# Two score products one place later, every sparse-attention softmax urgent, and wider value products in a hybrid decoder layer

## The chip, the cores and the metric

The kernel runs on one core of one Trainium2 chip. The metric is the device time of one execution in microseconds (us). The kernel before takes 330.74 us, the median of three runs (330.63 to 331.23). A lower time is better.

## The reference, cut to what matters

One decoder layer over 256 tokens of width 1024, in float32. Two causal attention mixers work side by side on the same normed input, and their outputs are concatenated into one output projection. Behind them stand a SwiGLU block, a gated per-layer embedding and a last norm, which the change does not touch.

```python
a = rmsnorm(h, g_attn[i])
proj = a @ w_in[i]
qa, ka, va, qi, ki, wi, qb, kb, vb = jnp.split(proj, offs, axis=-1)
...
y_a = dsa_attention(qa, ka, va, qi, ki, wi).reshape(B, L, W_DSA)
y_b = moba_attention(qb, kb, vb).reshape(B, L, W_MOBA)
h = h + jnp.concatenate([y_a, y_b], axis=-1) @ w_out[i]
f = rmsnorm(h, g_ffn[i])
h = h + (jax.nn.silu(f @ w_gate[i]) * (f @ w_up[i])) @ w_down[i]
```

Mixer A (called DSA) first scores every past key with a small indexer, keeps the 64 best keys of each query, and lets 8 query heads of 64 numbers attend to them. All 8 heads share one key head and one value head:

```python
rel = jax.nn.relu(jnp.einsum('bthd,bsd->bths', qib, k_idx).astype(jnp.float32))
score = jnp.einsum('bth,bths->bts', wb, rel)
score = jnp.where(causal[None], score, -jnp.inf)
_, idx = lax.top_k(score, top)
...
logits = jnp.where(valid[:, :, None, :], logits, -jnp.inf)
prob = jax.nn.softmax(logits, axis=-1).astype(v.dtype)
return jnp.einsum('bthk,btkd->bthd', prob, vs)
```

Mixer B (MoBA) is, at this length, plain causal attention of 8 heads, each with keys and values of its own.

## The kernel before, in words

TensorE (PE) runs in the order in which the program is written. The other engines run in an order that a planner settles when the kernel is built: by priority, which follows the order of the program text, and work written under `urgent()` comes 100 places earlier. On the chip each engine then takes its instructions in that settled order, one after the other.

A weight matrix comes in chunks of 1 MB. ScalarE (ACT) casts a chunk to `hi` (line 131), VectorE (DVE) subtracts to get the rest `lo` (line 159), and every product with weights is three matmuls, hi by hi, hi by lo and lo by hi (`mm3`, lines 176 to 178, or line 313 for the input projection).

The attention is cut into units. A unit is a kind (a for DSA, b for MoBA), a query tile of 128 tokens (t = 0 or 1) and the heads it takes: `A[0]` is tile 0 with all 8 heads and 128 keys, `A[1]` and `A[2]` are tile 1 with 4 heads each and 256 keys. A unit has three steps:

- `qk`: the score products (line 453) into two banks, one for even heads (e = 0) and one for odd heads (e = 1), and right behind them the softmax: DVE adds the mask and takes the minimum (line 471), ACT takes the exponential and its sum (line 477), DVE the reciprocal (481). Tile 0 is then scaled on DVE (484), tile 1 on ACT (488).
- `tp`: PE transposes the probabilities of one e (495), ACT copies them to `pT` (497).
- `pv`: products of the values with `pT` (509), even heads into partitions 0 to 63 of the bank and odd heads into 64 to 127. ACT and DVE take the result out as `yH` and `yL` (516, 517), which the output projection reads.

The mask of a DSA unit comes from `topk(t)` on DVE: eight rounds of the maximum of 8 (429) and its removal (430), and then lines 431 and 432 write `dmask`. `A[1]` and `A[2]` need the mask of tile 1.

These steps are put between the matmuls of the output projection by a plan: `at_tick(key, ...)` hangs functions on a place, and `tick(key)` runs them there. Place ("wb", n) lies behind the n-th group of six output products with MoBA's part of the weights (n = 0 to 3 for tile 0, 4 to 7 for tile 1), place ("wa", n) behind the n-th group of six with DSA's part for tile 0. Before, the softmaxes of `B[0]`, `A[1]` and `A[2]` are urgent (`first`, line 524), that of `A[0]` is not.

```python
        first = (B[0], A[1], A[2])
...
        at_tick(("wb", 0), A[0].qk, lambda: tp_rope(4, 1, qaT))
        at_tick(("wb", 2), B[2].pv, A[1].qk)
        at_tick(("wb", 5), tp(A[0], 0), tp(A[0], 1))
        at_tick(("wb", 6), A[0].pv, A[2].qk)
        at_tick(("wa", 0), tp(A[1], 0), tp(A[1], 1))
        at_tick(("wa", 1), A[1].pv)
```

`tp_rope(4, t, qaT)` transposes the rotated DSA queries of a tile on PE, and ACT copies them to `qaT` (381, 383). The score products of that tile read this copy.

Of the kernel before, what the change touches and what calls it, by code (L numbers as in the profile page):

```python
# [16 lines left out]
P = 128  # L17
# [45 lines left out]
def layer_kernel(  # L63
# [26 lines left out]
    def aux(name):  # L90
        return ps_aux.tile([P, NQ], F32, tag="aux", name=name)

    chunks, off = [], 0
    for kind, k0, nk, width, _, _ in CHUNKS:
        n = P * nk * width
# [84 lines left out]
    def urgent():  # L180
        return tc.high_priority(offset=URG)

    def tsl(t):
        return slice(t * P, (t + 1) * P)
# [87 lines left out]
    with actx:  # L272
# [105 lines left out]
        def transpose4(src, dstT, t, name):  # L378
            pt = aux(name)
            for b in range(4):  # L380
                nc.tensor.transpose(pt[:, b * P : (b + 1) * P], src[:, b * P : (b + 1) * P], ident)
            with urgent():
                nc.scalar.copy(dstT[:, :, tsl(t)], pt.rearrange("p (b n) -> p b n", b=4))
# [12 lines left out]
        def tp_rope(g, t, dstT):  # L396
            transpose4(ropes[(g, t)].rearrange("p h d -> p (h d)"), dstT, t, f"tr{g}{t}")
# [36 lines left out]
        class Unit:  # L434
# [57 lines left out]
            def tp(self, e):  # L492
                pt = aux(f"pt_{self.name}{e}")
                for b in range(4):
                    nc.tensor.transpose(pt[:, b * P : (b + 1) * P], self.pr[e][:, b * P : (b + 1) * P], ident)
                with urgent():
                    nc.scalar.copy(self.pT[:, e, :], pt)

            def pv(self):
                t, nb = self.t, self.nb  # L500
                ns = t + 1
                pv = aux(f"pv_{self.name}")
                for i in range(nb):
                    for s in range(ns):
                        for e in range(2):
                            hd = self.h0 + 2 * i + e
                            v = va[:, s, :] if self.kind == "a" else vb[:, s, hd * 64 : (hd + 1) * 64]
                            b = i * ns + s
                            nc.tensor.matmul(
                                pv[64 * e : 64 * e + 64, i * P : (i + 1) * P],  # L510
                                v, self.pT[:, e, b * P : (b + 1) * P], start=s == 0, stop=s == ns - 1,
                            )
                k0 = (0 if self.kind == "a" else 4) + self.h0 // 2
                src = pv[:, : nb * P].rearrange("p (k n) -> p k n", k=nb)
                with urgent():
                    nc.scalar.copy(yH[:, k0 : k0 + nb, tsl(t)], src)
                    nc.vector.tensor_tensor(
                        yL[:, k0 : k0 + nb, tsl(t)], src, yH[:, k0 : k0 + nb, tsl(t)].bitcast(F32), op=ALU.subtract
                    )

        B = [Unit("b", t, h0) for t, h0 in ((0, 0), (1, 0), (1, 4))]
        A = [Unit("a", t, h0) for t, h0 in ((0, 0), (1, 0), (1, 4))]

        first = (B[0], A[1], A[2])

        def at_tick(key, *fs):
            plan.setdefault(key, []).extend(fs)
# [13 lines left out]
        at_tick(("pp", 0), lambda: topk(1))  # L541
        at_tick(("pp", 1), tp(B[1], 0), tp(B[1], 1))
        at_tick(("pp", 3), B[1].pv, tp(B[2], 0), tp(B[2], 1), lambda: tp_rope(4, 0, qaT))
        at_tick(("wb", 0), A[0].qk, lambda: tp_rope(4, 1, qaT))
        at_tick(("wb", 2), B[2].pv, A[1].qk)
        at_tick(("wb", 5), tp(A[0], 0), tp(A[0], 1))
        at_tick(("wb", 6), A[0].pv, A[2].qk)
        at_tick(("wa", 0), tp(A[1], 0), tp(A[1], 1))
# [31 lines left out]
        qaT = at.tile([P, 4, 256], F32, tag="qaT", name="qaT")  # L580
# [36 lines left out]
        i = 0  # L617
# [28 lines left out]
    def trn(t, c, XHn, XLn, name):  # L646
        hg = hgs[(t, c)]
        pt = aux(f"ht_{name}{t}{c}")
        for b in range(4):
            nc.tensor.transpose(pt[:, b * P : (b + 1) * P], hg[:, b * P : (b + 1) * P], ident)  # L650
        pv = pt.rearrange("p (b n) -> p b n", b=4)
        kk = slice(4 * c, 4 * c + 4)
        with urgent():
            nc.scalar.copy(XHn[:, kk, tsl(t)], pv)
            nc.vector.tensor_tensor(XLn[:, kk, tsl(t)], pv, XHn[:, kk, tsl(t)].bitcast(F32), op=ALU.subtract)
# [48 lines left out]
    def hid_split(b, t, w, ht, H, L):  # L704
        nb = w // P
        pv = ht[:, :w].rearrange("p (s b i) -> p b s i", s=4, b=nb)
        kk = slice(4 * b, 4 * b + nb)
        hH = H[:, kk, tsl(t)].rearrange("p b (s i) -> p b s i", s=4)
        nc.scalar.copy(hH, pv)
        nc.vector.tensor_tensor(  # L710
            L[:, kk, tsl(t)].rearrange("p b (s i) -> p b s i", s=4), pv, hH.bitcast(F32), op=ALU.subtract
        )
# [232 lines left out]
```

## Time and profile before

| | |
|---|---|
| time, median of 3 runs | 330.74 us |
| the profiled execution | 330.68 us |
| its span, first to last instruction | 328.9 us |
| PE busy | 318.7 us, 97% of the span |
| DVE busy | 230.5 us, 70% |
| ACT busy | 181.5 us, 55% |
| granted TensorE clock, mean | 0.994 of full speed |

PE is at work nearly everywhere, so a wait of PE is time lost, and work of ACT or DVE costs only where PE waits for it. In rows of a timeline the first number is the start in us, the second the duration; the time in brackets is how long the engine had been idle, and what ended that. Matmuls and other instructions overlap their neighbours a little, so what one costs in a row of like ones is the step from its start to the next start, which is smaller than its duration.

### The profile page before, as it was taken

To read this page: it belongs to the slowest core of one execution; us is meant where nothing else is said; L and a number is where in the kernel's file an instruction comes from. 1 tells how busy PE (TensorE), PEld (TensorE's weight loads), DVE (VectorE), ACT (ScalarE), POOL (GpSimd) and SP (SyncE) were. 2 spreads that over 40 slices of the span, in tenths; PEclk is the share of its full clock that TensorE was granted. 3 is DMA by queue.
4 is the path that set the end of the run, shared out by engine and by line. 5 is a ranking of instruction groups with operands and counts; after the bars stand their busy time and mean duration, and the time that the engine had idled before them with its cause. 6 is when DMAs were issued, how large, how long until landed. Compare 5 with 4: busy or idle time off the path is not lost.

```text
span 328.9 us, 4397 instructions
## 1 busy us (share of the span) xinstructions
PE 318.7 (97%) x1589; PEld 260.0 (79%) x1589; DVE 230.5 (70%) x459; ACT 181.5 (55%) x294; POOL 6.1 (2%) x16
## 2 busy tenths in 40 slices
PE   8999999998989999999999999999999999999991
PEld 7888887776767788888888888888878888888891
DVE  4969999999966697547745756467573525279894
ACT  5966356898678495334543455335544333338533
POOL 2001000000000000000000000000000000000030
PEclk9999999999999999999999999999999999999997
DMA  7995948231503346677568476776858564551011
GB/s 257 417 392 221 369 157 299 87 129 40 217 5 125 129 148 251 241 271 259 170 253 295 149 286 236 262 248 212 250 169 313 210 209 175 190 192 66 0 64 65
DMA packets 19749, 66.00 MB, mean 201 GB/s; under 512 B 3344, under 2 KB 9488, under 8 KB 13456
## 3 DMA queue, kind: packets, MB, share of 16 engines
q1 hardware_dynamic: 19584, 65.53, 55.7%
q8 instruction: 12, 0.20, 0.3%
q10 hardware_dynamic: 144, 0.20, 0.2%
q14 instruction: 9, 0.07, 0.1%
HBM read 61.53 MB, written 4.19 MB: 200 GB/s over the span
## 4 chain that ended last, share of the span: by engine, by line
PE 83%; DVE 9%; ACT 6%; issue 0%
PE g L313 14%; PE ff L178 12%; PE ff L176 12%; PE ff L177 12%; PE wd L177 6%; PE wd L176 6%; PE wd L178 6%; PE pg L178 2%; PE pg L177 2%; PE pg L176 2%; DVE lo L159 2%; ACT pr_b L477 2%; DVE score L430 2%; ACT pr_a L477 2%; DVE m L429 1%; ACT hi L131 1%
## 5 line engine op out<-in xcount | busy, mean ns | idle before, releaser
L159 DVE TENSOR_TENSOR lo<-raw,hi 128x1024 fp32r<-128x1024 f32 (+1 forms) x99 | 116.8, 1207 | 62.8 <-ACT hi L131 62.8
L131 ACT CAST hi<-raw 128x1024 fp32r<-128x1024 f32 (+1 forms) x99 | 98.6, 1042 | 79.6 <-PE wd L178 31.9
L176 PE MATMUL ff<-hi,FH 128*128 128x512 f32 x176 | 68.7, 390 | 0.0
L178 PE MATMUL ff<-hi,FL 128*128 128x512 f32 x176 | 68.5, 389 | 0.0
L177 PE MATMUL ff<-lo,FH 128*128 128x512 f32 x176 | 68.5, 389 | 0.0
L178 PEld LDWEIGHTS ff<-hi,FL 128*128 128x128 f32 x176 | 33.0, 188 | 7.0
L177 PEld LDWEIGHTS ff<-lo,FH 128*128 128x128 f32 x176 | 33.0, 188 | 6.9
L176 PEld LDWEIGHTS ff<-hi,FH 128*128 128x128 f32 x176 | 33.0, 188 | 6.7
L177 PE MATMUL wd<-lo,hidH 128*128 128x512 f32 x88 | 35.1, 399 | 0.0
L176 PE MATMUL wd<-hi,hidH 128*128 128x512 f32 x88 | 34.9, 397 | 0.0
L178 PE MATMUL wd<-hi,hidL 128*128 128x512 f32 x88 | 34.5, 392 | 0.0
L313 PE MATMUL g<-hi,XH 128*128 128x512 f32 x64 | 25.5, 403 | 0.0
L313 PE MATMUL g<-hi,XL 128*128 128x512 f32 x64 | 24.8, 393 | 0.0
L313 PE MATMUL g<-lo,XH 128*128 128x512 f32 x56 | 21.7, 393 | 0.0
L176 PEld LDWEIGHTS wd<-hi,hidH 128*128 128x128 f32 x88 | 16.5, 188 | 4.4 <-DVE hid L749 0.3
L178 PEld LDWEIGHTS wd<-hi,hidL 128*128 128x128 f32 x88 | 16.5, 188 | 4.0
L177 PEld LDWEIGHTS wd<-lo,hidH 128*128 128x128 f32 x88 | 16.5, 188 | 3.7
L744 ACT ACTIVATE sg<-ff,f_y 128x512 f32<-128x512 f32 (+1 forms) x12 | 7.8, 647 | 15.0 <-PE ff L178 15.0
L749 DVE SCALAR_TENSOR_TENSOR hid<-ff,f_y,sg 128x512 f32<-128x512 f32 (+1 forms) x12 | 8.4, 703 | 10.5 <-PE ff L178 9.4
L313 PEld LDWEIGHTS g<-hi,XH 128*128 128x128 f32 x64 | 12.0, 188 | 3.1 <-issue 0.7
L313 PEld LDWEIGHTS g<-hi,XL 128*128 128x128 f32 x64 | 12.0, 188 | 2.6
L176 PE MATMUL pg<-hi,UH 128*128 128x512 f32 (+1 forms) x40 | 14.0, 349 | 0.0
(200 smaller groups left out, 441.7 us busy)
## 6 DMA issues: line engine op xcount, KB each, us to landing
raw<-in_w_dram SPq DMA_DIRECT2D x48, 1024.0 KB, 5.2
a<-in_xa_dram SPq DMA_DIRECT2D x8, 354.5 KB, 6.0
hidd<-hidb SPq DMA_DIRECT2D x11, 256.0 KB, 2.7
hidt<-hidd SPq DMA_DIRECT2D x44, 64.0 KB, 3.1
raw_g<-in_w_dram SPq DMA_DIRECT2D x2, 512.0 KB, 7.7
h<-in_x_dram SPq DMA_DIRECT2D x1, 1024.0 KB, 11.2
raw<-in_w_dram SPq DMA_DIRECT2D x2, 256.0 KB, 4.3
raw<-in_w_dram SPq DMA_DIRECT2D x1, 512.0 KB, 8.3
```

Of the source, the lines that this page charges most:

```text
L131: nc.scalar.copy(hi[:, o : o + step], raw[:, o : o + step])
L159: nc.vector.tensor_tensor(lo[:, o:e], raw[:, o:e], hi[:, o:e].bitcast(F32), op=ALU.subtract)
L176: nc.tensor.matmul(ps, aH, wH, start=start, stop=False)
L177: nc.tensor.matmul(ps, aH, wL, start=False, stop=False)
L178: nc.tensor.matmul(ps, aL, wH, start=False, stop=stop)
L313: nc.tensor.matmul(pss[t][:, :width], aT[:, k, tsl(t)], wT, start=k == 0 and n == 0, stop=k == KD - 1 and n == 2,)
L429: nc.vector.max(m8, s[:, :n])
L430: nc.vector.match_replace(s[:, :n], m8, s[:, :n], SENT)
L477: nc.scalar.activation(pr[:, sl], lg[:, sl], AF.Exp, bias=mn[:, j : j + 1], scale=-1.0, accum_out=su[:, j : j + 1])
L744: nc.scalar.activation(sg[:, :w], ps[:, :w], AF.Silu, scale=rf[t])
L749: nc.vector.scalar_tensor_tensor(hid[:, :w], up, rf[t], pgu[("s", t)][:, :w], op0=ALU.mult, op1=ALU.mult)
```

## The change

Three edits. The score products of `A[0]`, with the transposes of the second half of the DSA queries behind them, move from place ("wb", 0) to ("wb", 1), and those of `A[1]` from ("wb", 2) to ("wb", 3). The softmax of `A[0]` becomes urgent too. And `pv` of a DSA unit multiplies the values of a key tile with all its query blocks of one e in one matmul: `A[0]` has 2 matmuls of 512 columns where it had 8 of 128, `A[1]` and `A[2]` have 4 of 256 columns each where they had 8 of 128.

```diff
@@ -500,15 +500,17 @@
                 pv = aux(f"pv_{self.name}")
-                for i in range(nb):
+
+                wide = nb if self.kind == "a" else 1
+                for i in range(0, nb, wide):
                     for s in range(ns):
                         for e in range(2):
                             hd = self.h0 + 2 * i + e
                             v = va[:, s, :] if self.kind == "a" else vb[:, s, hd * 64 : (hd + 1) * 64]
-                            b = i * ns + s
+                            pT = self.pT[:, e, :].rearrange("p (i s n) -> p s i n", i=nb, s=ns)[:, s, i : i + wide, :]
                             nc.tensor.matmul(
-                                pv[64 * e : 64 * e + 64, i * P : (i + 1) * P],
-                                v, self.pT[:, e, b * P : (b + 1) * P], start=s == 0, stop=s == ns - 1,
+                                pv[64 * e : 64 * e + 64, i * P : (i + wide) * P],
+                                v, pT, start=s == 0, stop=s == ns - 1,
                             )
@@ -521,7 +523,7 @@
-        first = (B[0], A[1], A[2])
+        first = (B[0], *A)
@@ -541,8 +543,9 @@
-        at_tick(("wb", 0), A[0].qk, lambda: tp_rope(4, 1, qaT))
-        at_tick(("wb", 2), B[2].pv, A[1].qk)
+        at_tick(("wb", 1), A[0].qk, lambda: tp_rope(4, 1, qaT))
+        at_tick(("wb", 2), B[2].pv)
+        at_tick(("wb", 3), A[1].qk)
```

On DVE the edits change what stands between the softmax of `A[0]` and the end of the search for tile 1. Before, the last rows of the two run mixed; `m_1` and `score` with number 630 belong to the search of tile 1, `lg_a_1000` is a masked score of `A[0]`, odd heads, and `pr_a_989` its probabilities of even heads:

```order
L471 ISA lg_a_1000,mn_a_985<-qk_a_976,dmask 128x128
L471 ISA mn_a_985 128x1
L429 MAX m_1_876<-score_630 128x8
L481 RECIPROCAL rc_a_987<-su_a_986 128x4
L471 ISA lg_a_1000,mn_a_985<-qk_a_976,dmask 128x128
L471 ISA mn_a_985 128x1
L430 MATCH_REPLACE score_630<-m_1_876,score_630 128x256
L484 TENSOR_TENSOR pr_a_989<-pr_a_989,rc_a_987 128x512
L431 TENSOR_SCALAR dmask<-score_630 128x256
L517 TENSOR_TENSOR yL<-pv_b_1039,yH 128x2x128
L432 TENSOR_TENSOR dmask<-dmask,cadd 128x256
L471 ISA lg_a_1000,mn_a_985<-qk_a_976,dmask 128x128
```

Now all eight line-471 pairs of `A[0]` stand ahead of this piece, and from there DVE goes on as follows; `pr_a_995` and `pr_a_1007` are the probabilities of `A[0]`, even and odd heads, and `lg_a_1065` is the first masked score of `A[1]`:

```order
L429 MAX m_1_876<-score_630 128x8
L481 RECIPROCAL rc_a_993<-su_a_992 128x4
L430 MATCH_REPLACE score_630<-m_1_876,score_630 128x256
L484 TENSOR_TENSOR pr_a_995<-pr_a_995,rc_a_993 128x512
L429 MAX m_1_876<-score_630 128x8
L430 MATCH_REPLACE score_630<-m_1_876,score_630 128x256
L481 RECIPROCAL rc_a_993<-su_a_992 128x4
L519 TENSOR_TENSOR yL<-pv_b_1039,yH 128x2x128
L484 TENSOR_TENSOR pr_a_1007<-pr_a_1007,rc_a_993 128x512
L431 TENSOR_SCALAR dmask<-score_630 128x256
L432 TENSOR_TENSOR dmask<-dmask,cadd 128x256
L471 ISA lg_a_1065,mn_a_1062<-qk_a_1056,dmask 128x256
```

Two rounds of the search, both reciprocals of `A[0]` and both of its scalings (line 484) now stand between its scores and the mask of tile 1.

On ACT the order changes at the softmax of `A[2]`, between the value products of `A[0]` and those of `A[1]`. Before, with `pr_a_1135` and `pr_a_1144` the probabilities of `A[2]` and `pT_a_1077` the copy of the transposed probabilities of `A[1]`:

```order
L516 CAST yH<-pv_a_1114 128x4x128
L477 ACTIVATE pr_a_1135,su_a_1132<-lg_a_1134,mn_a_1131 128x256 x2
L477 ACTIVATE pr_a_1144,su_a_1132<-lg_a_1143,mn_a_1131 128x256
L488 ACTIVATE pr_a_1135<-pr_a_1135,rc_a_1133 128x256 x2
L477 ACTIVATE pr_a_1144,su_a_1132<-lg_a_1143,mn_a_1131 128x256
L497 COPY pT_a_1077<-pt_a_1173 128x512
L488 ACTIVATE pr_a_1144<-pr_a_1144,rc_a_1133 128x256 x2
L497 COPY pT_a_1077<-pt_a_1179 128x512
L131 CAST hi_1027<-raw_1025 128x1024 x2
```

Now, with `pr_a_1129` and `pr_a_1138` the probabilities of `A[2]` and `pT_a_1083` the copy of `A[1]`:

```order
L518 CAST yH<-pv_a_1114 128x4x128
L131 CAST hi_966<-raw_964 128x1024
L477 ACTIVATE pr_a_1129,su_a_1126<-lg_a_1128,mn_a_1125 128x256 x2
L477 ACTIVATE pr_a_1138,su_a_1126<-lg_a_1137,mn_a_1125 128x256 x2
L131 CAST hi_1027<-raw_1025 128x1024
L488 ACTIVATE pr_a_1129<-pr_a_1129,rc_a_1127 128x256 x2
L488 ACTIVATE pr_a_1138<-pr_a_1138,rc_a_1127 128x256 x2
L497 COPY pT_a_1083<-pt_a_1167 128x512
L497 COPY pT_a_1083<-pt_a_1173 128x512
```

A weight cast now stands on either side of `A[2]`'s exponentials, and both copies for `A[1]` stand behind all four scalings of `A[2]`.

## Rows read from the trace of the kernel before

**Rows 1.** Two lines of the page: busy time, share of the span and instructions of each engine, and the shares of the chain that ended last.

```profile
PE 318.7 (97%) x1589; PEld 260.0 (79%) x1589; DVE 230.5 (70%) x459; ACT 181.5 (55%) x294; POOL 6.1 (2%) x16
...
PE 83%; DVE 9%; ACT 6%; issue 0%
```

**Rows 2.** Waits of PE between 74 and 113 us, and, the last line, the only wait of its weight loads (PEld) from 115 us to the end. Columns: who waited, the releaser, us in total, times, longest us.

```profile
PE qk_a L453 <- ACT qaT L383: 1.0, 1, 1.0
PE pv_a L509 <- ACT pT_a L497: 0.9, 1, 0.9
...
PEld wd L176 <- DVE hid L749: 0.3, 1, 0.3
```

**Rows 3.** Timeline of PE at the scores of `A[0]` (16 records, 8 matmuls of 128 columns) and of `A[1]` (8 records, 4 matmuls of 256 columns).

```profile
79.44 0.39 PE L178 MATMUL wo<-hi,yL 128*128 128x512 f32 x1
80.84 1.16 PE L453 MATMUL qk_a<-idxT,qaT 64*128 64x128 f32 x16 [1.01 <-ACT qaT L383]
81.93 0.66 PE L381 MATMUL tr<-ident,qa 128*128 128x128 f32 x4
82.34 0.48 PE L176 MATMUL wo<-hi,yH 128*128 128x512 f32 x1
...
86.29 1.14 PE L453 MATMUL qk_a<-idxT,qaT 64*128 64x256 f32 x8
87.35 0.50 PE L176 MATMUL wo<-hi,yH 128*128 128x512 f32 x1
```

**Rows 4.** Timeline of PE at the value products of `A[0]` (94.95), `A[1]` (102.72) and `A[2]` (108.11).

```profile
93.69 0.39 PE L178 MATMUL wo<-hi,yL 128*128 128x512 f32 x1
94.95 1.57 PE L509 MATMUL pv_a<-pT_a,va 128*64 128x128 f32 x16 [0.87 <-ACT pT_a L497]
96.46 1.13 PE L453 MATMUL qk_a<-idxT,qaT 64*128 64x256 f32 x8
...
102.72 1.61 PE L509 MATMUL pv_a<-pT_a,va 128*64 128x128 f32 x16
104.26 0.50 PE L176 MATMUL wo<-hi,yH 128*128 128x512 f32 x1
...
108.11 1.09 PE L509 MATMUL pv_a<-pT_a,va 128*64 128x128 f32 x16
109.13 0.50 PE L176 MATMUL wo<-hi,yH 128*128 128x512 f32 x1
```

**Rows 5.** Timeline of DVE, from the last weight subtraction ahead of the softmax of `A[0]` to the first masked scores of `A[1]`.

```profile
81.89 1.21 DVE L159 TENSOR_TENSOR lo<-raw,hi 128x1024 fp32r<-128x1024 f32 x1
...
83.08 0.41 DVE L430 MATCH_REPLACE8 score<-m,score 128x256 f32<-128x256 f32 x1
83.41 0.28 DVE L471 CUSTOM_DVE_ANT_0 lg_a<-qk_a,dmask 128x128 f32<-128x128 f32 x1
...
83.61 0.42 DVE L429 MAX8 m<-score 128x8 f32<-128x256 f32 x1
...
86.24 0.16 DVE L481 RECIPROCAL rc_a<-su_a 128x4 f32<-128x4 f32 x1
...
86.90 0.68 DVE L484 TENSOR_TENSOR pr_a<-pr_a,rc_a 128x512 f32<-128x512 f32 x1
...
88.04 0.41 DVE L432 TENSOR_TENSOR dmask<-dmask,cadd 128x256 f32<-128x256 f32 x1
...
88.59 0.42 DVE L471 CUSTOM_DVE_ANT_0 lg_a<-qk_a,dmask 128x256 f32<-128x256 f32 x1
...
88.94 0.42 DVE L471 CUSTOM_DVE_ANT_0 lg_a<-qk_a,dmask 128x256 f32<-128x256 f32 x1
```

**Rows 6.** Timeline of ACT from the first query copy to the second copy of `A[1]`.

```profile
80.16 0.63 ACT L383 COPY qaT<-tr 128x512 f32<-128x512 f32 x1
...
83.73 0.40 ACT L477 ACTIVATE pr_a<-lg_a,mn_a 128x128 f32<-128x128 f32 x1 [0.52 <-DVE mn_a L471]
...
89.59 0.50 ACT L477 ACTIVATE pr_a<-lg_a,mn_a 128x256 f32<-128x256 f32 x1
...
90.08 0.39 ACT L477 ACTIVATE pr_a<-lg_a,mn_a 128x128 f32<-128x128 f32 x1
...
90.47 0.89 ACT L488 ACTIVATE pr_a<-pr_a,rc_a 128x256 f32<-128x256 f32 x2
...
93.39 1.03 ACT L131 CAST hi<-raw 128x1024 fp32r<-128x1024 f32 x1
94.33 1.06 ACT L497 COPY pT_a<-pt_a 128x512 f32<-128x512 f32 x2
95.28 1.05 ACT L131 CAST hi<-raw 128x1024 fp32r<-128x1024 f32 x1
...
101.35 0.56 ACT L497 COPY pT_a<-pt_a 128x512 f32<-128x512 f32 x1
...
102.62 0.57 ACT L497 COPY pT_a<-pt_a 128x512 f32<-128x512 f32 x1
```

**Rows 7.** Busy time of each engine in three stretches; the columns are named in the view as: us, PE busy (instructions), PEld, DVE, ACT, POOL, granted clock of PE, DMA share, GB/s.

```profile
74.00:84.00 10.00, 8.99 (x70) 7.25 (x69) 10.00 (x32) 8.12 (x16) 0.00 (x0) 1.00 0.31 102
...
320.00:325.00 5.00, 1.71 (x15) 1.50 (x13) 4.40 (x13) 2.67 (x4) 0.00 (x0) 1.00 0.13 48
325.00:329.00 4.00, 0.00 (x0) 0.00 (x0) 0.00 (x0) 0.00 (x0) 0.00 (x0) 0.51 0.36 133
```

## The prediction

> **What bounds the kernel now.** I read the page first: PE is busy for 318.7 of 328.9 us, and the chain that ended last is PE's for 83% [rows 1]. So the time is PE's work plus PE's waits. Next the waits of PE: in the attention part two are left, 1.0 us of the scores of `A[0]` for `qaT` and 0.9 us of the value products of `A[0]` for `pT`; from 115 us to the end there is one wait of 0.3 us [rows 2]. Two things follow. The change can win little more than these 1.9 us, and what it loses before 115 us arrives at the end in full, as no later wait is there to swallow it. Then the timelines of PE, DVE and ACT around the two places. One wait is not in the list of waits: the value products of `A[1]` take 1.54 us to the next start (102.72 to 104.26), those of `A[2]`, with both copies there, 1.02 us (108.11 to 109.13) [rows 4]. The missing 0.5 us are the second copy of `A[1]`, which starts at 102.62 [rows 6] while PE is already in the product.
>
> **The first place: the wait for `qaT` goes.** A like matmul of 512 columns steps by 0.23 us, so PE is free at 79.44 + 0.23 = 79.67, but the scores of `A[0]` start at 80.84 [rows 3], once the copy that started at 80.16 is done [rows 6]. Now the next group of six, 6 x 0.23 = 1.38, comes first, and by then, at 81.05, the copy is there. I let the change of operands cost 0.08, so the scores start at 81.13, take 1.09 (80.84 to 81.93), the transposes 0.41 (81.93 to 82.34), and PE is at the third group at 82.63. Before, the second group began at 82.34 and took 1.38 plus 0.10 for the first matmul behind another kind (0.48 against 0.39 in its row), so the third began at 83.8. That is 1.1 us won. The scores of `A[1]`, one place later, cut one more group from its neighbour, 0.1 to 0.2 us. So PE would be through its groups at 93.0 where it was at 93.69 + 0.23 = 93.92 [rows 4]: 0.9 us are in hand when it comes to the value products of `A[0]`.
>
> **The second place: the mask of tile 1 comes later.** On DVE, behind the subtraction at 81.89, come the removal at 83.08 and, now, a maximum and a removal that follow on each other (0.42 and 0.41 [rows 5], with the gaps between 0.9), so the first masked scores of `A[0]` start at 84.4 instead of 83.41. All eight then run in a row, 0.20 each (83.41 to 83.61), to 86.1. ACT takes the first exponential 0.32 behind its scores (83.41 to 83.73 [rows 5, 6]), at 84.7, then the second query copy (0.47), then seven more at 0.39 (90.08 to 90.47), to 88.3. The reciprocal of the even heads needs the fourth, with its sum ready at 86.9. From there DVE has, in order: two reciprocals (0.1 each; the one at 86.24 took 0.16 in all), two removals (0.40 each), one maximum that the second removal waits for (0.45), two scalings of line 484 (0.60 each), one `yL` of MoBA (0.34), lines 431 and 432 (0.77 with the wait of one for the other). The sum is 3.76 us, so the first masked scores of `A[1]` start at 90.65. Before, they started at 88.59, right behind line 432 at 88.04 [rows 5]. The mask of tile 1 is 2.1 us later, because the softmax that has just become urgent now stands ahead of it.
>
> **What that does to the value products of `A[0]`.** On ACT the softmax of `A[1]` and both copies of `A[0]` share one row. First exponential 0.47 behind the scores, 91.12; three at 0.49 (89.59 to 90.08) to 92.59; two scalings 0.80 (0.89 less the overlap) to 93.39; the fourth exponential to 93.88; the copy for the even heads to 94.36; two scalings to 95.16; the copy for the odd heads, done 0.57 later at 95.73 [rows 6]. Before, the two copies began at 94.33 and ended at 95.39. So the odd heads' copy, the later one, is 0.34 us later than before, though PE is there 0.9 us sooner. Before, the product ended 1.02 behind its odd copy (95.44 to 96.46); the wide one starts its odd half at 95.78 and, at the same speed per column, needs 1.0, so the scores of `A[2]` start at 96.78 and not at 96.46 [rows 4]. The 1.1 us are spent, with 0.3 on top.
>
> **What it does to `A[1]`'s value products.** Behind that product ACT has `yH` (0.49 from 96.94) and a weight cast, 0.94 (93.39 to 94.33 [rows 6]), which keep it to 98.4; the masked scores of `A[2]` follow `yL` at 98.4, so its exponentials begin at 98.9. Four take 1.96, the other weight cast 0.95, four scalings 1.60: 103.42. Only then come the copies for `A[1]`, 0.48 and 0.57, done at 104.47. Before, they started at 101.35 and 102.62 [rows 6], with one exponential, two scalings and no cast between. PE reaches this product at about 102.9 and has the second copy at 104.5. Before, the output products resumed 1.02 behind that copy (104.26 against 103.19 and 0.05 of notice [rows 4]); with the same 1.0 they resume at 105.53. That is 1.27 us. The same following of the rows, done for the kernel before, gives 104.35 for 104.26; I take 0.1 off: 1.2 us. Behind it nothing catches up: `A[2]`'s probabilities are scaled by 103.4, its copies (107.6 to 108.7) are done before PE gets to the product at 109.4, and the weight chunks that ride on these casts come long before their use.
>
> **The wide products.** The same columns pass, so I look at the nearest rows: the scores of `A[0]`, eight matmuls of 128, take 1.09 us, those of `A[1]`, four of 256, 1.06 [rows 3]. Those halves lie beside each other in the array by rows, these by columns; I take the one for the other. A unit made wide is thus worth 0.03, three units 0.1 at most; I take nothing, since two of the three wait for their odd half anyway. The other end: if the wide halves of even and odd heads did not overlap as the narrow ones do, `A[2]` would take up to 0.9 longer (its 1.02 less the edges, once more) and `A[1]`, whose odd half trails, 0.2: 1.1 in all. The scores with 256 columns, no slower than those with 128, speak against that.
>
> [...]
>
> **The sum.** 330.68 (the profiled execution) + 1.2 = 331.9 us; the median of the runs is 0.06 above that execution, which changes nothing.
>
> **Rivals.**
> 1. *The won microsecond stays, and it is faster.* The place is the second copy of `A[1]`. If it ended by 102.9, PE would wait nowhere after the first place but for the odd half of `A[0]`, and of the 1.1 us nearly all would arrive: 329.7. For it: two waits of PE are named and one is removed for certain. Against: ACT would have to be 1.5 us quicker between 91 and 104.5 than its rows, where it has hardly a gap. It decides at the mask: were `dmask` done at 88.45 as before, this would be the case.
> 2. *Only the first lateness is real.* The copies of `A[0]` are late by 0.3, but those of `A[1]` come within 0.5 of PE's arrival, because a cast or scaling overlaps better than I count. Then 330.68 + 0.0 to 0.6, say 330.9: no change that can be told. For it: 1.6 us of sums on two engines hang on each other. Against: ACT takes its row in order, and a cast and two scalings more are ahead of those copies.
> 3. *The wide halves run one after the other.* 331.9 + 1.1 = 333.0.
> 4. *TensorE's clock falls in the new waits.* PE would stand for about 1.4 us at 93.0 and 1.1 at 102.9. In the stretch with the wait of 1.0 us the granted clock was 1.00; at the end the last product ended at 321.7, and the clock was still 1.00 until 325 and at its lower level (0.51) after that [rows 7]. A gap of 1.4 us is thus far from what these rows show to lower it. If it fell, each us of PE work at the lower level would cost one more; for 2 us, 333.9.
>
> **How the numbers follow.** Chances: my forecast 0.66, rival 1 0.10, rival 2 0.17, rival 3 0.05, rival 4 0.02. The measurement of this kernel tells a difference of about 0.2%, 0.66 us, from none, so "same" ends at 331.4. Faster is rival 1, 0.10. Same is rival 2 and the lowest part of my forecast, 0.03: 0.20. Slower is the rest, 0.70. The forecast's own range is 331.4 to 332.4: each of its two sums has some fifteen steps read to 0.02. For 8 in 10 I go down into rival 2, to 330.8, and up to 332.5, short of rival 3.
>
> **What would show it.** In the profile after: no wait of `qk_a` for `qaT`, the scores of `A[0]` near 81.1. The first masked scores of `A[1]` on DVE near 90.6. The second `pT_a` copy of `A[0]` ending near 95.7, the copies of `A[1]` near 103.4 and 103.9, behind four scalings and a cast. PE waiting for `pT_a` twice, about 1.4 and 1.1 us, and the last product of the span 1.2 us later than 321.7. Wide value products of `A[2]` still near 1.0 us from their start to the next. The prediction is wrong if the copies of `A[1]` end before 103, or if the mask of tile 1 is done before 89.5.

## The result, and the profile after

The changed kernel takes 332.80 us, the median of six runs (332.27 to 333.15); the kernel before, 330.75 us in six runs (330.63 to 331.23). The ratio is 1.0056, its 95% interval 1.0043 to 1.0069: slower by 2.05 us. The forecast was 331.9 us with a range up to 332.5: the sign was right and the size too small.

To see where the time lies, I follow the starts of the same matmuls through both traces: the 61st record of PE, one that starts at 75.57 us before, ahead of all that the change touches, and one that starts at 167.44 us before, behind it. "Attention stretch" is the time from the second to the third, here and in the experiments. "Outside the span" is the measured time less the span from the first to the last instruction.

| us | before | after | more |
|---|---|---|---|
| to the 61st record | 10.77 | 11.24 | 0.47 |
| from there to the attention stretch | 64.80 | 64.80 | 0.00 |
| attention stretch | 91.87 | 93.23 | 1.36 |
| from there to the end of the span | 161.46 | 161.48 | 0.02 |
| outside the span | 1.78 | 2.15 | 0.37 |
| the profiled execution | 330.68 | 332.90 | 2.22 |

Only the 1.36 us in the attention lie where the change works. The other two parts are taken up below.

The page of after, for [rows 1]: PE is busy 1.2 us longer in a span that is 1.8 us longer.

```profile
PE 319.9 (97%) x1561; PEld 259.2 (78%) x1561; DVE 230.6 (70%) x459; ACT 180.7 (55%) x294; POOL 6.2 (2%) x16
...
PE 91%; ACT 4%; DMA 2%; DVE 1%; issue 1%; SPq 0%
```

Waits of PE of the kernel after, 74 to 113 us, for [rows 2]. It is the only line: the wait for `qaT` is gone, and the waits for `pT` have grown from 0.9 to 2.6 us.

```profile
PE pv_a L511 <- ACT pT_a L497: 2.6, 3, 1.4
```

Timeline of PE of the kernel after, for [rows 3] and [rows 4]: the scores of `A[0]`, its two wide products with a wait ahead of each, the scores of `A[2]`, the value products of `A[1]` and of `A[2]`, each with the output product behind it.

```profile
81.59 1.16 PE L453 MATMUL qk_a<-idxT,qaT 64*128 64x128 f32 x16
...
95.02 1.07 PE L511 MATMUL pv_a<-pT_a,va 128*64 128x512 f32 x2 [1.44 <-ACT pT_a L497]
96.30 1.07 PE L511 MATMUL pv_a<-pT_a,va 128*64 128x512 f32 x2 [0.21 <-ACT pT_a L497]
97.30 1.13 PE L453 MATMUL qk_a<-idxT,qaT 64*128 64x256 f32 x8
...
104.58 1.56 PE L511 MATMUL pv_a<-pT_a,va 128*64 128x256 f32 x8 [0.91 <-ACT pT_a L497]
106.07 0.50 PE L176 MATMUL wo<-hi,yH 128*128 128x512 f32 x1
...
109.95 1.08 PE L511 MATMUL pv_a<-pT_a,va 128*64 128x256 f32 x8
110.96 0.50 PE L176 MATMUL wo<-hi,yH 128*128 128x512 f32 x1
```

This trace is 0.47 us late before the change begins, so 0.47 is to be taken off each start. The output products then resume behind `A[1]` at 105.60, where they resumed at 104.26 [rows 4]: 1.34 us later. As in [rows 4], one wait has no bracket: the product of `A[1]` takes 1.49 us to the next start, that of `A[2]` 1.01, so some 0.5 us in it are its second copy.

DVE of the kernel after, for [rows 5]: the first masked scores of `A[0]`, the end of the mask of tile 1, the first masked scores of `A[1]`.

```profile
84.86 0.28 DVE L471 CUSTOM_DVE_ANT_0 lg_a<-qk_a,dmask 128x128 f32<-128x128 f32 x1
...
90.59 0.43 DVE L432 TENSOR_TENSOR dmask<-dmask,cadd 128x256 f32<-128x256 f32 x1
91.16 0.42 DVE L471 CUSTOM_DVE_ANT_0 lg_a<-qk_a,dmask 128x256 f32<-128x256 f32 x1
```

ACT of the kernel after, for [rows 6]: from the first exponential of `A[1]` to the two copies of `A[1]`.

```profile
91.63 0.51 ACT L477 ACTIVATE pr_a<-lg_a,mn_a 128x256 f32<-128x256 f32 x1 [2.52 <-DVE mn_a L471]
...
94.41 0.56 ACT L497 COPY pT_a<-pt_a 128x512 f32<-128x512 f32 x1
...
95.68 0.57 ACT L497 COPY pT_a<-pt_a 128x512 f32<-128x512 f32 x1
96.15 1.05 ACT L131 CAST hi<-raw 128x1024 fp32r<-128x1024 f32 x1
...
97.89 1.05 ACT L131 CAST hi<-raw 128x1024 fp32r<-128x1024 f32 x1
99.43 0.51 ACT L477 ACTIVATE pr_a<-lg_a,mn_a 128x256 f32<-128x256 f32 x1 [0.48 <-DVE mn_a L471]
...
101.42 1.03 ACT L131 CAST hi<-raw 128x1024 fp32r<-128x1024 f32 x1
102.36 1.70 ACT L488 ACTIVATE pr_a<-pr_a,rc_a 128x256 f32<-128x256 f32 x4
103.97 1.04 ACT L497 COPY pT_a<-pt_a 128x512 f32<-128x512 f32 x2
```

ACT stands still for 2.52 us until the mask of tile 1 and the first scores masked with it are done, and has hardly a gap from there to the copies of `A[1]`. Three casts and four scalings of `A[2]` stand between the copies of `A[0]` and those of `A[1]`.

### The profile page after: what moved, and what is told of

The parts are those of the page before. It is cut to its first block, busy times and chain, and to the rows that moved or that the text cites. A ratio compares the mean times of both kernels' runs of the same rounds, so it can differ in the third digit from the quotient of the medians.

```text
span 330.7 us, 4342 instructions
## 1 busy us (share of the span) xinstructions
PE 319.9 (97%) x1561; PEld 259.2 (78%) x1561; DVE 230.6 (70%) x459; ACT 180.7 (55%) x294; POOL 6.2 (2%) x16
## 4 chain that ended last, share of the span: by engine, by line
PE 91%; ACT 4%; DMA 2%; DVE 1%; issue 1%; SPq 0%
PE g L313 16%; PE ff L178 12%; PE ff L176 12%; PE ff L177 12%; PE wd L176 6%; PE wd L178 6%; PE wd L177 6%; PE pg L178 2%; PE pg L177 2%; PE pg L176 2%; PE wo L176 2%; PE wo L177 2%; PE wo L178 2%; DMA a<-in_xa_dram 2%; ACT pr_a L477 1%; PE qk_b L453 1%
```

## The experiments

The theory: the urgent softmax of `A[0]` delays the mask of tile 1 by 2.1 us, ACT is then behind with its row up to the copies of `A[1]`, and PE waits there. Rivals: the places or the wide products cost or win by themselves, the late mask is paid at the first value product already, or the clock falls in a wait.

**1. The urgent softmax alone.** In the kernel before:

```diff
-        first = (B[0], A[1], A[2])
+        first = (B[0], *A)
```

> Only the edit that makes the softmax of A[0] urgent; score products and value products as before. Theory 1 (the urgent softmax pushes the mask of tile 1 and reorders ACT, and this is the whole loss): the first masked scores of A[1] start near 90.6 us, the copies of A[1] near 104.0 and 104.5, PE waits for pT_a at A[0] and A[1], and the kernel is 1.8 us slower than before (332.5), more than with all three edits by the arithmetic of the queues. Theory 2 (the wide products cost the time that is over the forecast): about 1.2 us slower or less (331.9). Theory 3 (the later score products cost it): no change (330.7).

Measured: 333.61 us (332.88 to 334.70, six runs) against 331.05 of before (29 runs, shared with the next three): ratio 1.0080 [1.0063, 1.0097]; the attention stretch is 1.93 us longer. Its waits of PE:

```profile
PE pv_a L509 <- ACT pT_a L497: 2.9, 3, 1.5
PE qk_a L453 <- ACT qaT L383: 1.0, 1, 1.0
```

The old wait for `qaT` is still there, and the new ones for `pT` too. This one line makes the whole loss, and more. The largest time, 334.70, is the run with the lowest mean clock (0.989; the others have 0.993 to 0.996); experiments 8 to 10 come back to such runs.

**2. The places alone.** In the kernel before:

```diff
-        at_tick(("wb", 0), A[0].qk, lambda: tp_rope(4, 1, qaT))
-        at_tick(("wb", 2), B[2].pv, A[1].qk)
+        at_tick(("wb", 1), A[0].qk, lambda: tp_rope(4, 1, qaT))
+        at_tick(("wb", 2), B[2].pv)
+        at_tick(("wb", 3), A[1].qk)
```

> Only the two score products one place later; softmax of A[0] not urgent, value products as before. Theory 1 (the chain of softmax work on DVE and ACT sets when the value products of A[0] and A[1] can run): the wait for qaT of 1.0 us is gone, PE waits longer for pT_a instead, and the time stays within 0.2 us of before (330.7). The prediction's rival 1 (a microsecond is won where nothing else is late): 0.9 to 1.1 us faster (329.7). Theory 3 (the later places themselves cost time): slower by 0.5 us or more.

Measured: 331.01 us (12 runs), ratio 1.0000 [0.9992, 1.0009], attention stretch 91.87 us, as before to 0.01. The waits of PE show where the won microsecond went:

```profile
PE pv_a L509 <- ACT pT_a L497: 1.1, 1, 1.1
PE pt_a L495 <- DVE pr_a L484: 0.5, 1, 0.5
```

The 1.0 us for `qaT` are gone, and PE, earlier at the next two places, waits there: 0.5 us for the scaled probabilities, and 1.1 instead of 0.9 for `pT`. That is 0.7 of the 1.0 us; the rest was not followed.

**3. The wide products alone.** The first hunk of the change in the kernel before:

```diff
-                for i in range(nb):
+                wide = nb if self.kind == "a" else 1
+                for i in range(0, nb, wide):
...
-                                v, self.pT[:, e, b * P : (b + 1) * P], start=s == 0, stop=s == ns - 1,
+                                v, pT, start=s == 0, stop=s == ns - 1,
```

> Only the wide value products. Theory 1: within 0.1 us of before (330.7); the value products of A[2], whose copies are both there, still take about 1.0 us from their start to the next. Theory 2 (the wide products cost what was over the forecast): 0.5 to 1.1 us slower (331.2 to 331.8), and the value products of A[2] take 1.4 to 1.9 us.

Measured: 331.00 us (12 runs), ratio 1.0000 [0.9991, 1.0009]. The product of `A[2]` takes 1.01 us to the next start, before 1.02: the halves do not run one after the other.

**4. Places and wide products, softmax of `A[0]` not urgent.** In the kernel after:

```diff
-        first = (B[0], *A)
+        first = (B[0], A[1], A[2])
```

> The change without its urgent softmax: later places and wide products. Theory 1: as the places alone, within 0.2 us of before (330.6). Theory 2: slower than the places alone by 0.5 to 1.1 us. Theory 3: as slow as the places alone.

Measured: 331.02 us (12 runs), ratio 0.9999 [0.9990, 1.0008], attention stretch 91.86. With the urgent line away, the loss is away.

**5. The change again**, unedited.

> The change once more, to hold it against more runs of the kernel before. All theories: slower. Theory 1 (the rows of the attention part carry the whole loss): 1.4 us slower in the stretch between 75 and 170 us of the profile, as in the first profile, and the rest of the difference lies in the first 11 us, which come out differently from run to run also where the code there is the same, or outside the span. Theory 2 (a constant part at the start belongs to the change): the first 11 us are 0.5 us longer again.

Measured: 332.83 us (332.46 to 333.17, five runs) against 330.84 of before (15 runs, shared with the next three): ratio 1.0057 [1.0044, 1.0070]; attention stretch 93.20, 1.33 longer; 2.15 to 2.23 us outside the span. The 61st record starts at 11.21 us, again 0.44 later than in the one trace of before. The start does not belong to the change all the same: from 67 runs of before to 11 of the change the median span grows from 329.2 to 330.6 us, which is the attention's part alone.

**6. At which of the two products the late mask is paid.** In the kernel after, the softmax of `A[2]` is not urgent; that of `A[0]` still is, so the mask is as late:

```diff
-        first = (B[0], *A)
+        first = (B[0], A[0], A[1])
```

> The change, but the softmax of A[2] is not urgent, those of A[0] and A[1] are. The mask of tile 1 comes as late as in the change (first masked scores of A[1] near 90.6 us), but on ACT both copies of A[1] now stand ahead of the scalings of A[2]. Theory 1a (the loss is made at the second place, by what stands ahead of the copies of A[1] on ACT): copies of A[1] near 101.8 and 102.3, and the time of the kernel before within 0.3 us (331.0). Theory 1b (the late mask by itself is the loss, wherever it is paid): as slow as the change, 1.2 to 1.8 us over the kernel before.

Measured: 331.21 us (330.61 to 331.74, 11 runs), ratio 1.0009 [0.9999, 1.0019], attention stretch 91.75, 0.12 below before. The start of this trace agrees with that of before to 0.1 us, so starts compare directly. DVE, ACT and PE in its timelines:

```profile
90.59 0.42 DVE L471 CUSTOM_DVE_ANT_0 lg_a<-qk_a,dmask 128x256 f32<-128x256 f32 x1
...
101.75 1.06 ACT L497 COPY pT_a<-pt_a 128x512 f32<-128x512 f32 x2
102.70 0.92 ACT L488 ACTIVATE pr_a<-pr_a,rc_a 128x256 f32<-128x256 f32 x2
...
94.45 1.07 PE L511 MATMUL pv_a<-pT_a,va 128*64 128x512 f32 x2 [1.43 <-ACT pT_a L497]
...
96.74 1.13 PE L453 MATMUL qk_a<-idxT,qaT 64*128 64x256 f32 x8
...
103.01 1.08 PE L511 MATMUL pv_a<-pT_a,va 128*64 128x256 f32 x8
```

The masked scores of `A[1]` are as late as in the change (90.59; 91.16 less 0.47 there), and PE still waits 1.43 us at the product of `A[0]`. But the copies of `A[1]` now stand ahead of `A[2]`'s scalings, end at 102.8, and PE waits for nothing there. So the late mask eats the won microsecond at the first product and some 0.4 us more: with the 0.09 us added by which this trace starts earlier, the scores of `A[2]` start at 96.83, as in the change, and before at 96.46. The rest of the 1.36 us, some 1.0, is made at the second, by what ACT has ahead of these copies. The edit also takes away the wait for the second copy of `A[1]` that the kernel before has (0.5 us); whether it would win that without the urgent softmax of `A[0]` too was not run. The median still lies 0.37 us above that of before, and the time outside the span explains it: 2.14 us in the median here, 1.79 before.

**7. A shorter row on ACT.** Places and wide products, softmax of `A[0]` not urgent, and the probabilities of `A[1]` and `A[2]` are scaled on DVE:

```diff
-                    if t == 0:
+                    if t == 0 or self.kind == "a":
```

> Later places and wide products, softmax of A[0] not urgent, and the probabilities of A[1] and A[2] scaled on DVE in two wide passes instead of on ACT in four. If the row of ACT work between the mask and the copies sets the time (theory 1), eight scalings of 0.40 us less on ACT bring the copies of A[0] and A[1] 1.6 to 2.3 us forward, the wait for qaT is gone as well, and the kernel is 1.5 to 1.9 us faster than before (329.3). If PE waits for something else there, no gain (331.0).

Measured: 329.30 us (328.64 to 329.52, five runs), ratio 0.9953 [0.9939, 0.9967], attention stretch 89.77, 2.10 shorter. This version beats both kernels, by 1.5 and 3.5 us. PE waits for no `pT` any more; what is left of its waits in the attention is one of 0.5 us, and both copies of `A[1]` end at 101.1:

```profile
PE pt_a L495 <- DVE pr_a L484: 0.5, 1, 0.5
...
100.00 1.06 ACT L497 COPY pT_a<-pt_a 128x512 f32<-128x512 f32 x2
...
101.18 1.08 PE L511 MATMUL pv_a<-pT_a,va 128*64 128x256 f32 x8
```

**8. The change without wide products.** In the kernel after:

```diff
-                wide = nb if self.kind == "a" else 1
+                wide = 1
```

> The change without its wide products. Theory 1: the planner then puts both parts of a weight cast ahead of the yH of A[0] on ACT and the exponentials of A[2] begin 1.6 us later, near 100.5, so it is slower than the change by about 0.6 us (1.8 us over the kernel before), although the products themselves take the same. Theory 2 (wide products cost time): faster than the change by 0.5 to 0.8 us.

Measured: 334.90 us (333.53 to 335.24, five runs), ratio 1.0113 [1.0094, 1.0133]; attention stretch 95.40, 3.53 longer than before. Neither theory had this. PE in its timeline, from the product of `A[0]` to that of `A[1]`:

```profile
95.06 0.43 PE L511 MATMUL pv_a<-pT_a,va 128*64 128x128 f32 x2 [1.43 <-ACT pT_a L497]
96.34 1.29 PE L511 MATMUL pv_a<-pT_a,va 128*64 128x128 f32 x14 [0.84 <-ACT pT_a L497]
97.56 2.08 PE L453 MATMUL qk_a<-idxT,qaT 64*128 64x256 f32 x8
...
106.81 1.57 PE L511 MATMUL pv_a<-pT_a,va 128*64 128x128 f32 x16 [1.57 <-ACT pT_a L497]
```

The scores of `A[2]` take 2.08 us instead of 1.13. The reason is in the windows (columns as in [rows 7]):

```profile
94.00:97.00 3.00, 1.10 (x14) 0.86 (x15) 0.17 (x1) 3.00 (x8) 0.00 (x0) 1.00 0.00 0
97.00:101.00 4.00, 4.00 (x18) 2.62 (x15) 3.74 (x8) 1.65 (x3) 0.00 (x0) 0.57 0.15 23
```

and in the same windows of the kernel after:

```profile
94.00:97.00 3.00, 1.77 (x4) 0.38 (x4) 0.17 (x1) 3.00 (x8) 0.00 (x0) 1.00 0.00 0
97.00:101.00 4.00, 4.00 (x20) 2.86 (x20) 3.77 (x11) 3.30 (x10) 0.00 (x0) 1.00 0.00 0
```

The granted clock is 0.57 on the mean from 97 to 101 us here, and 1.00 in the change; from 88 to 97 and from 101 to 114 us it is 1.00 in both. A narrow product goes through even and odd heads in turn: its first matmul of 128 columns runs (0.43 us), and the second already waits for the odd copy. The wide one has 512 columns of the even heads to do in that time (1.07 us). So PE was busy for 1.10 of 3 us ahead of the fall, and for 1.77 in the change, where the clock stayed at 1.00. Ahead of the fall were two waits, 1.43 and 0.84 us.

**9 and 10. Which wide product keeps the clock up.** In the kernel after, only `A[0]` wide, and then only `A[1]` and `A[2]` wide:

```diff
-                wide = nb if self.kind == "a" else 1
+                wide = nb if self.kind == "a" and t == 0 else 1
```

```diff
-                wide = nb if self.kind == "a" else 1
+                wide = nb if self.kind == "a" and t == 1 else 1
```

> The change, with wide products for A[0] alone: those of A[1] and A[2] are 8 matmuls of 128 columns again. ACT and DVE have the same order as in the change, so only the products of A[1] and A[2] differ. Theory (with the waits on PE as they are, the wide product of A[0], which fills the time after the wait for pT at 95 us, is what keeps the clock at its upper level): no fall of the granted clock near 97 us, attention stretch 1.4 us longer than before as in the change, 332.8 us. Rival (any narrow value product behind a wait does it): a fall behind the product of A[1] near 105 us, 1 to 3 us more, 334 to 335.

> The change, with wide products for A[1] and A[2] alone: those of A[0] are 8 matmuls of 128 columns again. ACT and DVE have the same order as in the change without any wide product (two weight casts in a row behind A[0]'s yH). Theory (the narrow product of A[0] behind its wait lets the clock fall): the granted clock falls near 97 us as in the run without wide products, attention stretch 4 us longer than before, 334.5 to 335. Rival (the fall needs all three narrow products, or came by chance): no fall; the order on ACT alone makes the stretch 1.8 us longer, 333.0 to 333.3.

Measured with `A[0]` alone wide: 332.65 us (332.25 to 333.01, five runs) against 330.97 of before (23 runs, shared with the next three), ratio 1.0051 [1.0039, 1.0063], attention stretch 93.27: the change to 0.04 us. The narrow product of `A[1]`, behind its wait, does not lower the clock, which is 1.00 from 88 to 114 us:

```profile
104.02 1.57 PE L511 MATMUL pv_a<-pT_a,va 128*64 128x128 f32 x16 [0.92 <-ACT pT_a L497]
```

With `A[1]` and `A[2]` alone wide: 334.66 us (333.35 to 336.89, six runs), ratio 1.0115 [1.0087, 1.0142], attention stretch 95.41. PE in its timeline:

```profile
94.51 0.43 PE L511 MATMUL pv_a<-pT_a,va 128*64 128x128 f32 x2 [1.44 <-ACT pT_a L497]
95.79 1.65 PE L511 MATMUL pv_a<-pT_a,va 128*64 128x128 f32 x14 [0.84 <-ACT pT_a L497]
97.37 2.08 PE L453 MATMUL qk_a<-idxT,qaT 64*128 64x256 f32 x8
```

The same fall at the same place: the granted clock is 0.86 on the mean from 94 to 97 us and 0.68 from 97 to 101. So it is the product of `A[0]` that decides. The fall is not in every execution: the two runs with a mean clock of 0.993 and 0.994 took 333.35 and 333.55 us, the four with 0.985 to 0.989 took 334.54 to 336.89. In experiment 8, too, one run of five had 0.994 and took 333.53. What these three lie above the change, 0.55 to 0.75 us, may be the order on ACT that comes with the narrow product of `A[0]`: in both profiles one more weight cast stands ahead of `A[2]`'s exponentials, which in the change stands behind them. No profile of a run without the fall was kept, so that share is argued and not shown.

**11. Are the places worth anything?** The version of experiment 7 with the places of before:

```diff
-        at_tick(("wb", 1), A[0].qk, lambda: tp_rope(4, 1, qaT))
-        at_tick(("wb", 2), B[2].pv)
-        at_tick(("wb", 3), A[1].qk)
+        at_tick(("wb", 0), A[0].qk, lambda: tp_rope(4, 1, qaT))
+        at_tick(("wb", 2), B[2].pv, A[1].qk)
```

> The version with A[1] and A[2] scaled on DVE, wide products and no urgent softmax of A[0], but with the score products at their old places. Theory (the earlier score products win about 1 us on PE, which was lost again on ACT as long as ACT scaled; without the scalings it counts): the wait of the scores of A[0] for qaT is back, 1.0 us, and the time is 0.5 to 1.0 us above the version with the new places, 329.8 to 330.3. Rival (the places are worth nothing anywhere): 329.3 as that version.

Measured: 330.27 us (329.49 to 330.64, 12 runs), ratio 0.9977 [0.9968, 0.9986]; attention stretch 90.54, 0.77 longer than in experiment 7. Its waits of PE:

```profile
PE qk_a L453 <- ACT qaT L383: 1.0, 1, 1.0
PE pt_a L495 <- DVE rc_a L481: 0.5, 1, 0.5
```

With the scalings off ACT, the places win 0.8 us that they could not win in experiment 2.

**12. The whole change with the scaling on DVE.** The edit of experiment 7 in the kernel after, urgent softmax included.

> The whole change, the urgent softmax of A[0] included, with A[1] and A[2] scaled on DVE. Theory (the lateness of the mask is paid on ACT, and ACT's row is shorter by eight scalings): the copies of A[1] end near 102 us, before PE is there or just behind, attention stretch 0.9 us shorter than before, 329.8 to 330.3 us. Rival (the urgent softmax costs 1.4 to 1.9 us wherever the scaling is done): the version without it plus that, 330.7 to 331.3.

Measured: 330.44 us (330.07 to 330.88, 11 runs), ratio 0.9983 [0.9975, 0.9992]; attention stretch 91.11: 0.76 below before, near the theory's 0.9, and 1.34 above experiment 7, near the rival's 1.4. The median lies between the two ranges of times, just above the theory's. The copies of `A[1]` are done when PE comes to them, a little after the theory's 102, and still the urgent softmax costs as much as in the change. One wait of PE pays it, at the first product:

```profile
95.09 1.55 PE L511 MATMUL pv_a<-pT_a,va 128*64 128x512 f32 x4 [1.58 <-ACT pT_a L497]
...
101.68 1.06 ACT L497 COPY pT_a<-pt_a 128x512 f32<-128x512 f32 x2
102.86 1.08 PE L511 MATMUL pv_a<-pT_a,va 128*64 128x256 f32 x8
```

So the place where the late mask is paid depends on ACT's row: for the most part at the copies of `A[1]` in the change, at those of `A[0]` here. The price is the same: 1.34 us over the same version without the urgent line, in the change (93.20 against 91.86 in experiment 4) as here (91.11 against 89.77).

## Why the prediction was right about the way and wrong about the size

*The first place.* Right. The wait for `qaT` is gone; the scores of `A[0]` were forecast for 81.13, and 81.59 less 0.47 is 81.12.

*The mask of tile 1.* Right: forecast 90.65, found 91.16 less 0.47, 90.69.

*The value products of `A[0]`.* Right: the second copy ends at 96.25 less 0.47, 95.78 (forecast 95.73), and the scores of `A[2]` start at 96.83 (forecast 96.78). The first wait was 1.44 us for "about 1.4".

*The value products of `A[1]`.* The copies start at 103.50 where 103.42 was forecast. PE came a little later than reckoned, at 103.20 for 102.9, and waited 0.91 us where 1.1 was forecast. One reading of before was off, without effect on the sum: between the two copies stand two scalings only, and the exponential is ahead of the first. The rows gave 1.27 us for the output products behind it; then "I take 0.1 off: 1.2 us", because the same reckoning put the kernel before 0.09 us too late. Found were 1.34 at this place and 1.36 over the stretch. The correction went the wrong way, by a little.

*The wide products.* Taken as nothing, and alone they are nothing (experiment 3): `A[2]` takes 1.01 us to the next start where it took 1.02. The interval of experiment 3 begins at 0.9991, so at most 0.3 us can have been won there. What the prediction did not see is that in the change they are worth 2.1 us (332.8 against 334.9): without them the clock falls, to 0.57 on the mean from 97 to 101 us in experiment 8, and experiments 9 and 10 put that down to the product of `A[0]`. The runs without the fall leave some 0.7 of that to something else, probably the order on ACT.

*The sum.* This is the step that failed: "330.68 (the profiled execution) + 1.2 = 331.9 us". It carried everything outside the attention over from one execution of before. The attention is 0.16 us more than that sum had; the two parts that it put at nothing are larger. The first is the time outside the span, 2.14 to 2.24 us in all runs of the change where the execution of before had 1.78: 0.37 to 0.4 us that came with the change. Without them the time would have lain inside the range. The second is the start, and has nothing to do with the change. Over the 14 traces of this study the 61st record of PE starts anywhere from 10.6 to 11.8 us, with the same code up to there, and that execution, with 10.77, was one of the quicker ones; the later runs of before (29, 15 and 23) had medians of 331.05, 330.84 and 330.97, 0.16 to 0.37 above it. With 0.3 for this, 1.36 and 0.4 the sum is 332.7; the median is 332.8. All runs together say the same: between the medians of 67 runs of before and 11 of the change, the span grows by 1.4 us and the time outside it by 0.38.

*The rivals.* The won microsecond did not stay (1), since ACT's row was as full as its rows said; experiment 7 shows that it is to be had once that row is shorter. Only the first lateness real (2): no, the second one is (experiment 6). Wide halves one after the other (3): no (experiment 3). The clock (4): it did not fall in the change (1.00 from 94 to 101 us), but the argument against it, that a gap of 1.4 us is far from what lowers it, is refuted by experiments 8 and 10, where behind 1.43 or 1.44 and 0.84 us, with a short matmul between, it was 0.57 and 0.68 on the mean from 97 to 101 us. Its chance was set too low for a bad reason: that the clock stayed up in the change is owed to the wide product of `A[0]`, which the prediction took as worth nothing, and so was luck.

## What to carry to other kernels

Making a unit urgent makes another late: before raising a priority, find what now stands behind it on that engine and which wait of the bottleneck engine hangs on that; here one line lost 2 us in a change whose other two parts lost nothing. If an earlier start is worth nothing, look for the engine whose row is full between the two waits, and shorten that row. And add a forecast of one microsecond to the median of many executions, not to one, with the parts that vary from execution to execution, and the time outside the span, named.

## What the runs showed of the hardware

**The clock can fall behind two waits that are each short.** In experiment 10 it was 0.68 on the mean from 97 to 101 us, in the change 1.00. The longest wait ahead of the fall was 1.44 us, as long as one in the change. What differed was the work between the waits, 128 columns instead of 512, and with it the second wait, 0.84 us instead of 0.21. In the profile of experiment 1, with the same narrow product between waits of 0.54 and 0.85 us, no such fall shows: the scores of `A[2]` took 1.13 us there, 2.08 in experiment 10, and the mean clock of that execution is 0.996, against 0.989. In the window from 94 to 97 us PE was busy for 1.10 us in experiment 8 and for 1.77 in the change; by what rule the clock falls was not shown.

**The start varies.** The first product with weights took 0.50 us to the next start before, and 0.88 after, in the same code. PE before:

```profile
4.33 0.66 PE L313 MATMUL g<-ahi,XH 128*128 128x452 f32 x2
4.83 0.60 PE L313 MATMUL g<-alo,XH 128*128 128x452 f32 x2
```

and after:

```profile
4.43 1.04 PE L313 MATMUL g<-ahi,XH 128*128 128x452 f32 x2
5.31 0.57 PE L313 MATMUL g<-alo,XH 128*128 128x452 f32 x2
```

In both traces the granted clock is 1.00 there. Why was not tried.

**Time outside the span goes with the kernel, not only with the run.** It was 1.74 to 1.87 us in the kernel before and in experiments 2 to 4, where the softmax of `A[0]` is not urgent, and 2.10 to 2.24 in the change and in experiments 1, 5, 6 and 8 to 10, where it is. Experiment 1 differs from before by that one line, so as long as ACT does the scaling the line brings these 0.4 us too. With the scaling on DVE it does not go by the line: 1.84 to 1.91 with it (experiment 12), 1.74 to 2.16 without (7 and 11). What happens in this time no trace shows, so a fifth of the loss that was measured is put to a line and not to a mechanism.
